# Block sums of the squared ReLU formed and stored by the first feed-forward product

## The chip, the cores and the metric

The kernel runs on one core of a Trainium2 chip. Its time is the device time of one execution in microseconds. Five engines work side by side: TensorE (matrix products), VectorE and ScalarE (element by element), GpSimd (also called POOL in the profile) and SyncE (SP), which here issues every transfer between the core's memory and the chip's large memory.

## The reference

One trunk layer of a streaming encoder on an input of 1024 frames with 1024 channels: an RWKV-7 branch and a convolution branch, merged under gates, and then a feed-forward part. Only that last part is touched:

```python
h2 = _rmsnorm(x, norm_ff_g[l])
x = x + jnp.square(jax.nn.relu(h2 @ w_ff1[l])) @ w_ff2[l]   # 1024 -> 4096 -> 1024 channels
return _rmsnorm(x, norm_final_g)
```

The second product sums over the 4096 hidden channels, so their order is free as long as the rows of `w_ff2` follow it.

## The kernel before

Everything is kept with the channels across the 128 partitions and the frames along them. A tile is 128 channels by 1024 frames; most instructions take half of one, 128 x 512. Float32 values are multiplied as two parts: `parts_of_` (L1306) lets ScalarE write the first part and VectorE or GpSimd the second, the low one, as the difference. A product of two such numbers is three matmuls. `low_engine` (L1302) gives every `lows[0]`-th low part to GpSimd and the rest to VectorE; in the second product `LOW4 = 3` makes it every third. The weights are split in `halved` (L1196), with the low part always on GpSimd.

Large products use seven block products instead of eight (`seven`, L1247). The right side is cut in two halves of its channels and two halves of the frames, B11, B12, B21 and B22, and the products need the differences T1 = B12 - B11, T2 = B22 - T1, T3 = B22 - B12 and T4 = B21 - T2 as well. In code `less` (L1313) forms one on VectorE. Weights have their own four sums (`weight_sums`, L1213), also on VectorE. A block product runs over four blocks of 128 x 128 weights and so takes twelve matmuls.

The first feed-forward product makes 32 tiles of hidden channels: four one by one (`single`, L1701), while the blocks of h are being formed in `h_blocks` (L1648), and 28 in fourteen pairs (`f_pair`, L1728). ScalarE applies ReLU and the square, and `store_f` (L1634) stores each half tile in `f_d`. Results lie in a pool of four work tiles (`wkt`, L1159).

The second product takes the hidden channels in eight groups of four tiles. `prepare` (L1759) loads the eight half tiles of a group, forms four differences for each of two pairs of tiles, and splits all blocks in two parts in `places`. `quad` (L1815) is the unit of work: seven products of twelve matmuls for four tiles of output; two quads make a group, and there are fourteen quads. VectorE adds every result to x, which lies in the tiles `C`. The eighth group is done directly (`last_group`, L1880), and needs its blocks without differences. The first group is prepared during the last pair (`last_pair`, L1740).

`prepare`, `h_blocks` and the like are generators in a list called `background`; one or two steps of the first in the list are traced after every three matmuls. `Count.until` (L1316) makes a step wait for a number of these. TensorE keeps the order in which the code is traced. The other engines did until line 1152, where `order_off` ends that; after it a scheduler at build time fixes their order from the dependencies and the trace order, so a transfer or a sum can be placed well ahead of the place where it is traced. At run time every engine, and SP with its transfers, goes through its own list in order.

Of the kernel before, what the change touches and what calls it, by code (L numbers as in the profile page):

```python
# [44 lines left out]
LOW4 = 3  # L45
# [49 lines left out]
def tile_hybrid_block(ctx: ExitStack, tc: tile.TileContext, xT, win, wap, wcp, wop, wf1, wf2,  # L95
# [3 lines left out]
    class Ordered:  # L99
        """While on, the instructions of an engine keep the order in which they are traced;  # L100
        work: how long they take, in ns."""
# [109 lines left out]
    def load_weight(src):  # L211
        """src: DRAM AP [128, 4, 128]; the transfer, then (second call) the split into two
        float32r parts whose sum it is."""
        raw = wp.tile([P, 4, P], F32, tag="raw", name="raw")
        sync.dma_start(raw, src)

        def halve():
            hi = wp.tile([P, 4, P], F32R, tag="whi", name="whi")
            lo = wp.tile([P, 4, P], F32R, tag="wlo", name="wlo")
            act.activation(hi, raw, AF.Copy)  # L220
            eng = pool if nload[0] % 2 else dve
            nload[0] += 1
            eng.tensor_tensor(out=lo, in0=raw, in1=hi.bitcast(F32), op=ALU.subtract)
            return hi, lo

        return halve
# [9 lines left out]
    def stream(pick):  # L236
        """Matrix products unit after unit, the weights of a part loaded ahead[0] parts before
        and split ahead[1] parts before; yields True after every three products, False when no
        unit can start. pick() names the next unit, WAIT for none now, None at the end. A unit:
        (wsrc [128, 8, 128] in DRAM, rhs(kt, seg) -> (hi, lo), evac(seg, psum), segs, what to  # L240
        trace after which of its yields), or a function that returns the list of its parts, or
        one that returns a generator (its first two steps load and prepare). A part: what traces
        its load and returns what traces its split; the generator of its products from the split
        weights, which yields what follows. What follows a product on other engines is traced
        after the next products."""
# [54 lines left out]
        def fetch():  # L300
            """Entries ahead of the one in work, no more than one of them WAIT."""
# [53 lines left out]
    def pick():  # L355
        """The first of the queue whose time has come."""
# [26 lines left out]
    def rms_scale(acc, eps):  # L383
        """acc [128, SEG], per-partition partial sums of squares, becomes 1/sqrt(mean + eps) on all partitions."""
# [29 lines left out]
    def early_unit(n):  # L414
        """Gate logits of the first half of the frames from x with its gain; then the scale of the frames."""
# [102 lines left out]
    H0, H1 = slice(0, 64), slice(64, 128)  # L518
    with ExitStack() as st:
# [17 lines left out]
        # ----- low-rank branches: first layer, the token shift folded into the weights  # L537
# [51 lines left out]
        def decay_and_a():  # L589
# [3 lines left out]
            # the two parts of the second layer's weights stacked over the contraction  # L593
# [54 lines left out]
        # ----- r, k, v with their token shift  # L648
# [26 lines left out]
        # ----- one step: head pair p, token segment s; i = 2 p + s  # L675
# [17 lines left out]
        # the parts of a step are generators: one stage a tick, a stage uses what other  # L693
        # engines made in the stages before
# [146 lines left out]
        # inverse of I - L: the 16 x 16 diagonal blocks by substitution, one block a partition  # L841
        def invert(i):
# [48 lines left out]
            # the blocks of 32 and of 64 from their halves  # L891
# [30 lines left out]
        # then the blocks of 32 and of 64 from their halves  # L922
# [11 lines left out]
        def chain(i):  # L934
            """The chunks of a step one after another; yields after each group of products."""
# [88 lines left out]
        # ----- conv branch and the merge gates  # L1024
# [25 lines left out]
        def conv(p, u):  # L1050
            """The even and the odd frames are each a filter of 16 taps over the even frames of u
            and one of 15 over the odd ones; what the odd frames need follows from the filter of
            the sums over the sum of both, less the two products that the even frames need."""
# [37 lines left out]
        # ----- the order of the products: chains of small ones among the large  # L1091
# [79 lines left out]
    # work of the other engines, traced in small steps between the products  # L1171
# [14 lines left out]
    # Two halves of the rows B of the right side (its channels) and of its columns (the frames):  # L1186
    # T1 = B12 - B11, T2 = B22 - T1, T3 = B22 - B12, T4 = B21 - T2; of the weights, by pairs of
    # tiles of output channels: S1 = A21 + A22, S2 = S1 - A11, S3 = A11 - A21, S4 = A12 - S2.
    # The products in their order: A11 B11, S1 T1, S2 T2, A12 B21, S3 T3, S4 B22, A22 T4.
    # seven places, each for a block of four tiles of half the frames in two parts  # L1190
# [5 lines left out]
    def halved(src, eng=pool):  # L1196
        """Two float32r parts of [128, 4, 128] whose sum is src."""
# [8 lines left out]
    def raw_tile(n):  # L1206
        """The n-th of eight places [128, 4, 128] for weights."""
# [5 lines left out]
    def weight_sums(srcs, base):  # L1213
        """What traces the loads and what the splits of the weights of the seven products."""
# [32 lines left out]
    def seven(srcs, base, blocks, pairs, evacs, hook):  # L1247
        """Parts of a unit: the seven products of one pair of tiles (or of two of half as many channels)."""
# [3 lines left out]
        # two pairs: the sums that are done at once before those that stay  # L1252
# [21 lines left out]
    def four(emit, place):  # L1274
        """What follows each of the seven products; emit(tile, half of the frames, place or None, values)."""
# [30 lines left out]
    def parts_of_(z, src):  # L1306
        """Generator: src as the sum of its two parts z."""
# [8 lines left out]
    class Count:  # L1316
        """Yields of the products so far; hooks wait for them."""
# [14 lines left out]
    # conv: LayerNorm, swish, block sums  # L1332
# [4 lines left out]
    def conv_branch():  # L1337
# [44 lines left out]
        for j in range(4):  # L1382
            for kt in (j, 4 + j):
                # c_d has the even frames, then the odd ones; from here on in order
# [42 lines left out]
    # A  # L1427
# [29 lines left out]
    # A @ W_A under its gate  # L1457
# [33 lines left out]
    # the merged branches: y in the places of C  # L1491
# [15 lines left out]
    def y_blocks():  # L1507
        """The block sums of y, as their places and the last tiles of y come."""
        B = [C[j] + C[4 + j] for j in range(4)]     # b11, b12, b21, b22; then t2, t3, t4, b22
# [61 lines left out]
    # x1 = x + y @ W_out, in the same places  # L1571
# [24 lines left out]
    # the first hidden channels come from x1 under its gain, the scale of the frames later  # L1596
# [34 lines left out]
    f_d = [dtile(f"f_d{i}", [P, T]) for i in range(4 * NK)]  # L1631
    FO = (4, 5, 6, 0, 2, 1, 3)

    def store_f(i, s, t):  # L1634
        sync.dma_start(f_d[i][:, s * SEG : (s + 1) * SEG], t)
# [12 lines left out]
    def h_blocks():  # L1648
# [30 lines left out]
        for j in range(4):  # L1679
            yield from parts_of_(FP[6][j], C[4 + j][0])  # L1680
        yield from at_F.until(16 * NCL + 56)
        for m in range(NK):
            for h in range(NSEG):
                sync.dma_start(C[m][h], x1_d[m][:, h * SEG : (h + 1) * SEG])
                yield

# [14 lines left out]
    def single(i):  # L1701
        """Parts of a tile of hidden channels, the last frames first."""
# [25 lines left out]
    def f_pair(n, i, hook):  # L1728
        def emit(j, s, t, src):
            if t is None:  # L1730
                t = wkt("c21")
# [4 lines left out]
        return lambda: pair(wf1, n, i, i + 1, [PL[z] for z in FO], emit, lambda i, s: wkt("c"), hook)()  # L1736
# [3 lines left out]
    def last_pair():  # L1740
        if at_L.n == 0:
            drain()
            lows[0] = LOW4
            background.append(prepare(0))
        at_L.hook()
# [4 lines left out]
    # back to the channels of x, 4 tiles of the hidden channels at a time  # L1750
    NG = 8
# [7 lines left out]
    def prepare(g):  # L1759
        """The blocks of group g of hidden channels, of two tiles each; of the last group B11, B12, B21, B22."""  # L1760
        z = places(g)
        FB[g] = [[(z[4 * j + 2 * k], z[4 * j + 2 * k + 1]) for k in range(2)] for j in range(7)]
        raw = {}

        def load(k):
            for a, kk in ((1, k), (2, 2 + k)):
                for s in range(NSEG):
                    t = raw[k, a, s + 1] = wkt("fl") if g and k == 0 else flt("fl")
                    sync.dma_start(t, f_d[4 * g + kk][:, s * SEG : (s + 1) * SEG])

        def free(i):
            """The place of block i of group 0 has been read by the last products of the hidden channels."""
            return at_L.until(4 * (i // 2 + 1) if g == 0 else 0)

        load(0)
        yield
        if g:
            load(1)
            yield
        for k in range(2):  # L1780
            if k == 1 and g == 0:
                load(1)
                yield
            b11, b12, b21, b22 = (raw[k, a, s] for a in (1, 2) for s in (1, 2))
# [193 lines left out]
```

## Time and profile before

| | us |
|---|---|
| median of 3 runs (2221.46 to 2228.85) | 2223.68 |
| span of the profiled execution, first to last instruction | 2220.0 |
| TensorE busy in it | 2075.3 (93%) |
| VectorE busy | 1617.9 (73%) |
| ScalarE busy | 1120.3 (50%) |
| GpSimd busy | 898.0 (40%) |

The profile is of one execution. Busy time is a sum over the whole span, so a stage in which VectorE has no idle time does not show in it; windows do that. In rows, PE is TensorE, DVE is VectorE, ACT is ScalarE; `c<-c,x` means that the instruction writes a tile named c from a tile c and a tile x. Names repeat with the tile pools: `place` and `a` are the places of the blocks, `fl` and `c` tiles loaded from `f_d` or the tiles of x, `cmean` two more tiles of x, `raw` and `s` weights and their sums, `x` and `g` the accumulators of TensorE. In windows, PEclk is the granted TensorE clock as a share of 2.4 GHz.

### The profile page before, as it was taken

To read this page: it belongs to the slowest core of one execution; us is meant where nothing else is said; L and a number is where in the kernel's file an instruction comes from. 1 tells how busy PE (TensorE), PEld (TensorE's weight loads), DVE (VectorE), ACT (ScalarE), POOL (GpSimd) and SP (SyncE) were. 2 spreads that over 40 slices of the span, in tenths; PEclk is the share of its full clock that TensorE was granted. 3 is DMA by queue.
4 is the path that set the end of the run, shared out by engine and by line. 5 is a ranking of instruction groups with operands and counts; after the bars stand their busy time and mean duration, and the time that the engine had idled before them with its cause. 6 is when DMAs were issued, how large, how long until landed. Compare 5 with 4: busy or idle time off the path is not lost. (4 is left out here: it accounts for less than half of the span.)

```text
span 2220.0 us, 35280 instructions
## 1 busy us (share of the span) xinstructions
PE 2075.3 (93%) x12806; PEld 1554.3 (70%) x12806; DVE 1617.9 (73%) x2781; ACT 1120.3 (50%) x2102; POOL 898.0 (40%) x1026
## 2 busy tenths in 40 slices
PE   6999999999999999999989989799899998889897
PEld 4757666767676666676666778577688876667686
DVE  8435889869778888898484987979432249998865
ACT  7454555555555555654323753455555555333323
POOL 4103333333333333342112245665545456566641
PEclk8999999999999999999999999999899999999999
DMA  5243222222222222232254355242433334233212
GB/s 180 90 158 79 62 73 53 80 65 78 78 66 79 72 81 72 74 87 82 70 178 159 128 170 163 95 137 93 169 105 114 105 106 151 91 95 105 85 49 76
DMA packets 223358, 224.87 MB, mean 101 GB/s; under 512 B 113488, under 2 KB 131408, under 8 KB 223184
## 3 DMA queue, kind: packets, MB, share of 16 engines
q1 hardware_dynamic: 223184, 222.62, 32.3%
q8 instruction: 101, 1.65, 0.3%
q14 instruction: 73, 0.60, 0.1%
HBM read 155.96 MB, written 66.60 MB: 100 GB/s over the span
## 5 line engine op out<-in xcount | busy, mean ns | idle before, releaser
L114 POOL TENSOR_TENSOR wlo<-raw,whi 128x512 fp32r<-128x512 f32 x258 | 369.4, 1434 | 698.9 <-ACT whi L114 640.1
L114 PE MATMUL g<-hhi,whi 128*128 128x512 f32 x912 | 402.9, 442 | 0.0
L114 PE MATMUL g<-hhi,wlo 128*128 128x512 f32 x912 | 363.4, 398 | 2.1 <-POOL wlo L114 1.5
L114 PE MATMUL g<-hlo,whi 128*128 128x512 f32 x912 | 364.8, 400 | 0.0
L114 ACT ACTIVATE whi<-raw 128x512 fp32r<-128x512 f32 x328 | 204.5, 625 | 222.4 <-PE g L114 73.0
L114 PEld LDWEIGHTS g<-hhi,whi 128*128 128x128 f32 x912 | 173.1, 190 | 52.4 <-issue 6.0
L114 PE MATMUL x<-place,whi 128*128 128x512 f32 x608 | 195.5, 403 | 14.8 <-DVE cmean L114 7.8
L114 PE MATMUL x<-a,whi 128*128 128x512 f32 x544 | 177.2, 408 | 33.3 <-ACT c L114 11.3
L114 PE MATMUL g<-place,whi 128*128 128x512 f32 x624 | 198.8, 399 | 7.6 <-ACT place L114 4.1
L114 PEld LDWEIGHTS g<-hhi,wlo 128*128 128x128 f32 x912 | 174.4, 191 | 44.5 <-POOL wlo L114 2.4
L114 PE MATMUL g<-a,whi 128*128 128x512 f32 x624 | 196.9, 397 | 5.7 <-DVE c L114 3.3
L114 PEld LDWEIGHTS g<-hlo,whi 128*128 128x128 f32 x912 | 174.1, 191 | 26.6 <-issue 1.9
L114 DVE TENSOR_TENSOR c<-c,g 128x512 f32<-128x512 f32 (+1 forms) x131 | 84.6, 650 | 94.8 <-PE g L114 94.6
L114 PEld LDWEIGHTS x<-a,whi 128*128 128x128 f32 x544 | 105.2, 196 | 63.0 <-ACT c L114 12.7
L114 PEld LDWEIGHTS x<-place,whi 128*128 128x128 f32 x608 | 115.1, 192 | 48.1 <-issue 6.2
L114 POOL TENSOR_TENSOR wlo<-s,whi 128x512 fp32r<-128x512 f32 x72 | 107.5, 1495 | 100.1 <-ACT whi L114 91.8
L114 PEld LDWEIGHTS g<-place,whi 128*128 128x128 f32 x624 | 118.2, 190 | 38.6 <-ACT place L114 5.0
L114 PEld LDWEIGHTS g<-a,whi 128*128 128x128 f32 x624 | 117.7, 190 | 35.7 <-DVE c L114 4.6
L114 POOL TENSOR_TENSOR tmpb<-lb,xb 64x15 f32<-64x15 f32 (+7 forms) x240 | 110.2, 459 | 79.3 <-DMA lb<-scr_l 63.2
L114 ACT ACTIVATE stw<-stv,wc 64x64 f32<-64x64 f32 x240 | 82.6, 344 | 97.7 <-DVE stv L114 94.2
L114 PE MATMUL g<-a,wlo 128*128 128x512 f32 x312 | 123.4, 396 | 5.6 <-POOL wlo L114 5.2
L114 PE MATMUL g<-place,wlo 128*128 128x512 f32 x312 | 123.6, 396 | 1.6 <-POOL wlo L114 1.6
(286 smaller groups left out, 4327.6 us busy)
## 6 DMA issues: line engine op xcount, KB each, us to landing
raw<-wf SPq DMA_DIRECT2D x128, 256.0 KB, 2.8
raw<-win SPq DMA_DIRECT2D x124, 256.0 KB, 3.1
f_d<-c SPq DMA_DIRECT2D x56, 256.0 KB, 2.0
fl<-f_d SPq DMA_DIRECT2D x46, 256.0 KB, 2.9
c<-f_d SPq DMA_DIRECT2D x18, 256.0 KB, 3.3
xt<-xT SPq DMA_DIRECT2D x16, 256.0 KB, 5.3
ga_d<-gt SPq DMA_DIRECT2D x16, 256.0 KB, 2.1
z_d<-za SPq DMA_DIRECT2D x16, 256.0 KB, 2.0
```

The lines of the kernel that those rows point to most:

```text
L114: ins = f(*a, **k)
```

## The change

`f_d` becomes one tensor for each pair of tiles, with a place for every block: B11, T1, T2, B21, T3, B22, T4. `store_f` stores B11, B21 and B22 as they come; once all four halves of a pair are there, `f_sums` is put at the head of the background. After four steps it forms the four differences in place on VectorE, one a step, and stores each. For the last group the four blocks alone are stored. `prepare` loads each block ready made and only splits it, block by block in the order of use, with loads six blocks ahead (three in the first group). `LOW4` is so large that all of its low parts go to VectorE.

The results of the pairs come to lie in a ring of eight tiles, those of C[4] to C[7], instead of the four work tiles, as soon as `h_blocks` has ended; x1 is loaded back into these eight during the last pair, and only into C[0] to C[3] at the earlier place. A group's two tile pairs are now neighbours, so the rows of `w_ff2` are permuted on the host.

```diff
-LOW4 = 3
+LOW4 = 1 << 30
...
-    f_d = [dtile(f"f_d{i}", [P, T]) for i in range(4 * NK)]
+    NP = 2 * NK
+    NG = 8
+    f_d = [dtile(f"f_d{k}", [7 if k // 2 < NG - 1 else 4, P, SEG]) for k in range(NP)]
     FO = (4, 5, 6, 0, 2, 1, 3)
+    FT = [{} for _ in range(NP)]
 
     def store_f(i, s, t):
-        sync.dma_start(f_d[i][:, s * SEG : (s + 1) * SEG], t)
+        k, a = divmod(i, 2)
+        f = FT[k]
+        f[a, s] = t
+        if k // 2 == NG - 1:
+            sync.dma_start(f_d[k][2 * a + s], t)
+            return
+        if (a, s) != (0, 1):
+            sync.dma_start(f_d[k][{(0, 0): 0, (1, 0): 3, (1, 1): 5}[a, s]], t)
+        if len(f) == 4:
+            background.insert(0, f_sums(k))
+
+    def f_sums(k):
+        b11, b12, b21, b22 = (FT[k][a, s] for a in range(2) for s in range(2))
+        for _ in range(4):
+            yield
+        for n, out, x, y in ((1, b11, b12, b11), (4, b12, b22, b12), (2, b22, b22, b11), (6, b21, b21, b22)):
+            less(out, x, y)
+            sync.dma_start(f_d[k][n], out)
+            yield
...
+        ring.extend(C[m][h] for m in range(4, NK) for h in range(NSEG))
         yield from at_F.until(16 * NCL + 56)
-        for m in range(NK):
+        yield from x1_back(range(4))
+
+    ring = []
+
+    def x1_back(ms):
+        for m in ms:
             for h in range(NSEG):
                 sync.dma_start(C[m][h], x1_d[m][:, h * SEG : (h + 1) * SEG])
                 yield
+
+    def ft():
+        if not ring:
+            return wkt("c")
+        ring.append(ring.pop(0))
+        return ring[-1]
...
             if t is None:
-                t = wkt("c21")
+                t = ft()
...
-        return lambda: pair(wf1, n, i, i + 1, [PL[z] for z in FO], emit, lambda i, s: wkt("c"), hook)()
+        return lambda: pair(wf1, n, i, i + 1, [PL[z] for z in FO], emit, lambda i, s: ft(), hook)()
...
             drain()
+            ring.clear()
             lows[0] = LOW4
             background.append(prepare(0))
+            background.append(x1_back(range(4, NK)))
...
+        items = [(j, k) for j in range(7 if g < NG - 1 else 4) for k in range(2)]
         raw = {}
+        LA = 6 if g else 3
+
+        def load(n):
+            j, k = items[n]
+            raw[n] = wkt("fl") if g and n % 2 else flt("fl")
+            sync.dma_start(raw[n], f_d[2 * g + k][j])
+
+        for n in range(LA):
+            load(n)
         yield
...
+        yield
+        for n, (j, k) in enumerate(items):
+            if n + LA < len(items):
+                load(n + LA)
+
+            yield from at_L.until(4 * (j // 2 + 1) if g == 0 else 0)
+            yield from parts_of_(FB[g][j][k], raw.pop(n))
...
-        "wop": wl(a(w_out)[0]), "wf1": wl(a(w_ff1)[0]), "wf2": wl(a(w_ff2)[0]),
+        "wop": wl(a(w_out)[0]), "wf1": wl(a(w_ff1)[0]), "wf2": wl(a(w_ff2)[0].reshape(8, 2, 2, P, 1024).transpose(0, 2, 1, 3, 4).reshape(4096, 1024)),
```

## Rows read from the trace of the kernel before

**Rows 1.** Windows: from:to, length, busy us (count) of each engine, clock, DMA share, GB/s.

```profile
1504.91:1568.82 63.91, 53.31 (x208) 40.82 (x206) 57.33 (x61) 36.59 (x63) 33.99 (x23) 0.87 0.32 107
1584.83:1817.19 232.36, 232.36 (x1010) 189.33 (x1008) 68.14 (x85) 126.81 (x216) 111.43 (x84) 1.00 0.32 109
1817.19:1840.06 22.87, 19.89 (x85) 15.63 (x84) 16.81 (x20) 15.20 (x29) 13.85 (x9) 1.00 0.36 119
1840.06:2157.16 317.10, 286.90 (x1177) 222.49 (x1176) 276.64 (x366) 116.74 (x205) 194.06 (x133) 0.97 0.30 96
2118.91:2157.16 38.25, 38.25 (x169) 31.54 (x168) 25.58 (x38) 11.98 (x20) 20.88 (x16) 1.00 0.17 56
```

**Rows 2.** Waits of TensorE, fourteen quads: total us, times, longest.

```profile
PE x L114 <- DVE cmean L114: 12.8, 6, 3.9
PE g L114 <- DVE c L114: 4.3, 4, 1.8
...
PE x L114 <- DVE c L114: 3.5, 5, 1.6
```

**Rows 3.** Waits of TensorE from the single tiles to the end of the first pair.

```profile
PE x L114 <- ACT c L114: 7.6, 1, 7.6
```

**Rows 4.** Instruction groups of VectorE, fourteen quads: busy us, mean ns, idle before.

```profile
L114 DVE TENSOR_TENSOR place<-fl,place 128x512 fp32r<-128x512 f32 x28 | 26.2, 940 | 0.8 <-ACT place L114 0.8
L114 DVE TENSOR_TENSOR a<-fl,a 128x512 fp32r<-128x512 f32 x21 | 23.7, 1129 | 0.0
L114 DVE TENSOR_TENSOR fl<-fl 128x512 f32<-128x512 f32 x24 | 22.3, 928 | 0.6 <-POOL place L114 0.6
L114 DVE TENSOR_TENSOR raw<-raw,raw 128x512 f32<-128x512 f32 x14 | 17.8, 1268 | 5.4 <-POOL wlo L114 5.4
L114 DVE TENSOR_TENSOR raw<-raw,s 128x512 f32<-128x512 f32 x14 | 16.2, 1157 | 3.8 <-POOL wlo L114 3.8
L114 DVE TENSOR_TENSOR s<-s,raw 128x512 f32<-128x512 f32 x13 | 14.0, 1077 | 0.0
L114 DVE TENSOR_TENSOR s<-raw 128x512 f32<-128x512 f32 x13 | 12.2, 936 | 17.4 <-POOL wlo L114 10.3 <-DMA raw<-wf 7.1
L114 DVE TENSOR_TENSOR fl<-c,fl 128x512 f32<-128x512 f32 x12 | 10.3, 857 | 0.0
...
L114 DVE TENSOR_TENSOR place<-c,place 128x512 fp32r<-128x512 f32 x10 | 8.7, 874 | 0.0
L114 DVE TENSOR_TENSOR fl<-fl,fl 128x512 f32<-128x512 f32 x6 | 5.9, 982 | 0.0
L114 DVE TENSOR_TENSOR c<-c,fl 128x512 f32<-128x512 f32 x7 | 5.2, 749 | 0.0
L114 DVE TENSOR_TENSOR a<-c,a 128x512 fp32r<-128x512 f32 x4 | 3.5, 881 | 0.0
```

**Rows 5.** Instruction groups of GpSimd, fourteen quads: low parts of blocks alone.

```profile
L114 POOL TENSOR_TENSOR place<-fl,place 128x512 fp32r<-128x512 f32 x14 | 21.1, 1512 | 14.4 <-ACT place L114 13.4 <-PE x L114 0.8
L114 POOL TENSOR_TENSOR a<-fl,a 128x512 fp32r<-128x512 f32 x11 | 16.4, 1490 | 14.0 <-ACT a L114 11.2 <-DVE fl L114 1.8 <-PE x L114 0.9
L114 POOL TENSOR_TENSOR place<-c,place 128x512 fp32r<-128x512 f32 x5 | 6.6, 1314 | 6.2 <-ACT place L114 6.2
...
L114 POOL TENSOR_TENSOR a<-c,a 128x512 fp32r<-128x512 f32 x2 | 3.0, 1515 | 0.7 <-ACT a L114 0.7
```

**Rows 6.** Instruction groups of VectorE, twelve pairs of the first product.

```profile
L114 DVE TENSOR_TENSOR s<-s,raw 128x512 f32<-128x512 f32 x12 | 21.4, 1784 | 0.0
...
L114 DVE TENSOR_TENSOR s<-raw 128x512 f32<-128x512 f32 x12 | 8.3, 693 | 19.7 <-DMA raw<-wf 19.7
```

**Rows 7.** Transfers of the tensor f_d, the same twelve pairs, all stores.

```profile
DMA to landing us min/median/max: 2.0/2.0/3.6
```

**Rows 8.** Waits of the SP queue, fourteen quads.

```profile
SPq L114 <- POOL wlo L114: 140.1, 42, 10.1
```

**Rows 9.** Waits of VectorE, fourteen quads.

```profile
DVE s L114 <- DMA raw<-wf: 7.1, 3, 4.5
```

More of the change, by code (lines that the diff above doesn't have):

```diff
@@ L1748, in tile_hybrid_block @@
         program.append(f_pair(n, i, at_F.hook if i < 30 else last_pair))
-    NG = 8
     ODD = NCL // 2 % 2
@@ L1762, in prepare @@
         FB[g] = [[(z[4 * j + 2 * k], z[4 * j + 2 * k + 1]) for k in range(2)] for j in range(7)]
+        items = [(j, k) for j in range(7 if g < NG - 1 else 4) for k in range(2)]
         raw = {}
[L1765 to L1775, printed above, removed]
-        yield
[L1777 to L1784, printed above, removed]
-            if g == NG - 1:
-                for j, b in enumerate((b11, b12, b21, b22)):
-                    yield from parts_of_(FB[g][j][k], b)
-                continue
-            yield from free(0)
-            yield from parts_of_(FB[g][0][k], b11)
-            t1 = b11
-            less(t1, b12, b11)
-            yield
-            yield from free(1)
-            yield from parts_of_(FB[g][1][k], t1)
-            less(b12, b22, b12)
-            yield
-            t2 = t1
-            less(t2, b22, t1)
-            yield
-            yield from free(2)
-            yield from parts_of_(FB[g][2][k], t2)
-            yield from free(3)
-            yield from parts_of_(FB[g][3][k], b21)
-            less(b21, b21, t2)
-            yield
-            yield from free(4)
-            yield from parts_of_(FB[g][4][k], b12)
-            yield from free(5)
-            yield from parts_of_(FB[g][5][k], b22)
-            yield from free(6)
-            yield from parts_of_(FB[g][6][k], b21)
+        LA = 6 if g else 3
[5 more added lines that the diff above has]
+            load(n)
+        yield
+        yield
[4 more added lines that the diff above has]
+            yield from parts_of_(FB[g][j][k], raw.pop(n))
     def quad(g, q):
```

## The prediction

> **What bounds the kernel now.** I read the page first. TensorE is busy nearly everywhere, so only the stages where it loses time can give any back. So the next view was a table of windows, cut where the timeline of matmuls shows a unit of seven products begin [rows 1]. Its five lines are: the four single tiles of the first feed-forward product and the first two products of its first pair; twelve of its fourteen pairs; its last pair; the fourteen quads of the second product; and the last two quads alone. The reader is to see three things.
>
> The first product runs without a gap: twelve pairs in 232.36 us, 19.36 us each, with TensorE busy throughout at clock 1.00 (2.4 GHz) and VectorE busy for only 68.14 us [rows 1].
>
> The second product has as many matmuls in a quad as a pair has, and takes 317.10 us for fourteen. At 19.36 us each it would take 271.1, so 46.0 us are lost, part of them as a lower clock (mean 0.97) after stalls. VectorE is busy for 276.64 of the 317.10 us, 87.2% [rows 1]. The waits of TensorE there name VectorE's accumulations into the rows of x (12.8, 4.3 and 3.5 us) ahead of anything else [rows 2]. The check is the last two quads: there only eight blocks are prepared, and those of the last group without differences; VectorE falls to 25.58 of 38.25 us and the two quads run at 19.1 us each [rows 1]. So VectorE is the bound of the second product, and it stops being one somewhere between 67% and 87%.
>
> Around the second product two more places lose time: the last pair takes 22.87 us, 3.5 over [rows 1], and the change from single tiles to pairs has one stall of 7.6 us, on ScalarE's copy out [rows 3]. In that stretch VectorE is busy for 57.33 of 63.91 us [rows 1].
>
> **The change part by part.** *Differences leave the second product.* VectorE forms them today from the loaded tiles: 24, 12, 6 and 7 instructions that write fl or c from fl and c, 43.7 us in the stretch of fourteen quads [rows 4]. (There are 56; the other seven fall in the last pair.) All go: -43.7 us of VectorE.
>
> *Every low part goes to VectorE.* In the same stretch GpSimd does 14 + 11 + 5 + 2 = 32 of them, 47.1 us [rows 5]. VectorE's own 63 cost 26.2 + 23.7 + 8.7 + 3.5 = 62.1 us, 0.986 each [rows 4]. A moved one costs between 0.69 us, which a subtraction takes when nothing holds it (0.693), and 1.78 us, which the one that starts beside a GpSimd instruction takes in the first product (1.784) [rows 6]. I take 0.986, the same operation in the same stage: 32 x 0.986 = +31.5 us.
>
> *Less collision.* VectorE's weight sums have a mean of 1.08 to 1.27 us where most are long and 0.94 where they are not [rows 4], against 0.69 free [rows 6]: 54 of them (60.2 us) lose 22.9 us. The 63 low parts lose 62.1 - 63 x 0.69 = 18.6, and the 49 differences 43.7 - 33.8 = 9.9. Together 51.4 us beside 133 GpSimd instructions [rows 1], 0.39 us for each. With 32 fewer: -12.5 us. The bounds are 0 and twice that.
>
> Sum for VectorE: -43.7 + 31.5 - 12.5 = -24.7 us, so 276.6 becomes 251.9. At the busy share of today (87.2%) the stretch takes 251.9 / 0.872 = 289 us, 28 less. The bounds: all moved parts held and no relief, -43.7 + 57.0 = +13.3, which is 15 us longer; none held and double relief would put it below TensorE's 271.1, so at most 46.0 shorter. I take 29, a little over the sum, because ScalarE's first parts no longer stand behind a difference on VectorE.
>
> The Trainium skill, on the page SBUF — State Buffer, section Who interferes with whom, has the rule behind these two prices: a VectorE instruction with two SBUF inputs and a GpSimd instruction that reads SBUF exclude one another, and the second one waits for the whole of the first. The trace agrees (0.693 against 1.784). Read strictly it speaks against this change: the moved parts join the side that waits, while the weights' low parts stay on GpSimd. That is the second rival below.
>
> *The last pair.* The preparation of the first group goes on there, and loses its seven differences; its low parts on GpSimd come over. I take -2 of the 3.5 us that are lost; 0 and 3.5 are the ends.
>
> *Differences enter the first product.* Twelve pairs get four each, 48 instructions, 33 us at 0.69 and 85 at 1.78 [rows 6]. VectorE is idle there for 232.36 - 68.14 = 164 us [rows 1], in gaps behind TensorE's products, so I cost them at nothing. They write in place, over tiles whose plain store must have landed: 2.0 us in the median, 3.6 at most [rows 7]. If VectorE sits in such a wait, an accumulation behind it is late and a bank is not freed; the ring of eight tiles and the four steps of delay are the cover. If it is gone, a pair loses about one product, 19.36 / 7 = 2.8 us, 33 us over twelve pairs. GpSimd's 84 weight parts (111.43 us [rows 1]) can be held too; they have as much room again. Nothing below zero is to be had, since TensorE has no gap there.
>
> *The single tiles.* Two pairs of tiles get their differences while the blocks of h are formed: eight more instructions, 5.5 us at 0.69 to 14.2 at 1.78, in a stretch with 63.91 - 57.33 = 6.6 us of idle VectorE [rows 1], on the path to the stall of 7.6 us [rows 3]. Also, all four work tiles are held until the differences are stored, and the first pair's copy takes one of them. Ends: 0 and +14. I take +6, close to the free price. Against it, eight of the sixteen reloads of x1 leave that stretch for the end of the first product; I count nothing for them.
>
> *Transfers.* Six more quarter-megabyte transfers a group each way on the SP queue. DMA share is 0.30 to 0.32 now [rows 1], so bytes cost nothing; the order of the queue is the third rival. The weight rows are permuted on the host: nothing.
>
> Sum: -29 - 2 + 0 + 6 = -25 us on a span of 2220.0, so 2195. The median of the runs shown lies 3.7 above that span, which gives **2199 us**.
>
> **The rivals.** *TensorE becomes the bound.* VectorE's load falls far enough that the second product and the last pair run without gaps, as the last two quads do now [rows 1]: -46.0 - 3.5 and no cost at the single tiles, 2174 us. For it: a group then has no chain of differences between load and block. Against it: 251.9 us of VectorE in 271.1 is 93%, more than today's share.
>
> *VectorE stays the bound.* The lock takes back what the count gives: moved parts at 1.2 us, halfway between the two prices [rows 6], and no relief, -43.7 + 38.4 = -5.3, 6 us gained. The single tiles cost the same 6, and the last pair gains nothing: 2224 us. For it: the count falls only from 366 to 349 instructions. Against it: the same operation costs 0.986 now, with more GpSimd work beside it.
>
> *The SP queue turns the second product slower.* A group has fourteen block loads instead of eight between its eight weight loads. A block load waits until the low part that last read its tile is done; all those are now on the busiest engine, and a weight load queued behind it comes late. SP already waits for 140.1 us on GpSimd's weight parts, and VectorE's sums wait for a weight load 3 times, 7.1 us in all, 4.5 the longest [rows 8, 9]. It decides from 25 / 14 = 1.8 us a quad. At 2.4 us, the mean of those three, fourteen quads lose 33 and the change ends 8 above the median, 2232 us; at 4.5 it is 2262. Against it: eight tiles and six loads ahead, and ScalarE and VectorE need no chain before they free one. The Trainium skill, on the page DMA: Bandwidth & Descriptors, section Anatomy of one DMA — SWDGE (gpsimd) path, says that the wait for a semaphore happens on the issuing sequencer before dispatch; by it every load behind the waiting one is held, as this rival needs.
>
> *The first product is no longer free,* and the differences only move the loss: 33 us, as worked out above, so 2199 + 33 = 2232 us.
>
> **How the numbers follow.** Forecast 0.52 (2188 to 2212), TensorE bound 0.18, VectorE still bound 0.15, SP queue 0.10, first product held 0.05. A change of 0.3% is 6.7 us, about what can be told from none here. Faster by more: the forecast, the first rival and a third of the second, 0.75. Slower by more: most of the last two, 0.13. The rest, 0.12, is no change. The range reaches from the TensorE bound to just past the second rival, 2176 to 2228.
>
> **What would show it.** Right: quads of the middle groups at 20 to 21 us instead of 22 to 24, VectorE near 250 us in the second product with no instruction that writes fl from fl, GpSimd at about 101 instructions, pairs still at 19.4 us. The step of the single tiles is right if the stall before the first pair grows by about 6 us and wrong if it shrinks. The price of a moved part is read from the mean of VectorE's low parts: near 1.0 or below supports the sum, 1.2 or more the second rival. Gaps in the pairs, or sums that wait for weight loads in most quads, would make the prediction wrong.

## The result, and the profile after

The changed kernel takes 2190.38 us in the median (2188.81 to 2192.52, 4 runs) against 2222.57 for the kernel before beside it: ratio 0.9862, 95% interval 0.9839 to 0.9885. Run again with later experiments it gave 2187.1 us, ratio 0.9852 (0.9829 to 0.9874). The forecast was 2199 us in a range of 2176 to 2228.

The spans of the profiled executions, 2220.0 and 2187.1 us, differ by 32.9 us. Cut at the same units of work as [rows 1], they compare like this:

| stage | before, us | after, us | difference | forecast |
|---|---|---|---|---|
| up to the single tiles | 1504.91 | 1504.92 | 0.0 | 0 |
| single tiles and first pair | 79.92 | 84.22 | +4.3 | +6 |
| twelve pairs | 232.36 | 232.40 | 0.0 | 0 |
| last pair | 22.87 | 23.63 | +0.8 | -2 |
| fourteen quads | 317.10 | 279.43 | -37.7 | -29 |
| last group and end | 62.84 | 62.50 | -0.3 | 0 |

Of the 37.7 us that the quads gain, 25.6 are idle time of TensorE that is gone; the other 12.0 are TensorE's own time for the same matmuls, 286.90 us [rows 1] and 274.87 now, with a mean granted clock of 0.97 before and 0.99 after.

The windows of the changed kernel, cut as in [rows 1] and with the same columns (the busy times are TensorE, its weight loads, VectorE, ScalarE, GpSimd):

```profile
1504.92:1573.71 68.79, 52.57 (x208) 40.80 (x206) 61.27 (x68) 36.88 (x63) 38.20 (x24) 0.90 0.34 115
1589.14:1821.54 232.40, 232.40 (x1009) 189.56 (x1008) 130.65 (x132) 126.80 (x216) 114.76 (x84) 1.00 0.45 153
1821.54:1845.17 23.63, 21.49 (x85) 16.81 (x84) 17.02 (x23) 18.66 (x34) 8.46 (x7) 0.93 0.82 266
1845.17:2124.60 279.43, 274.87 (x1178) 221.41 (x1176) 248.96 (x343) 114.79 (x199) 143.23 (x101) 0.99 0.46 140
```

In the second line VectorE goes from 68 to 131 us and TensorE still has no gap. In the fourth VectorE is at 248.96 us with 343 instructions and GpSimd at 101 instructions; the forecast had 251.9 and 101. Of the fourteen quads the first three take 20.7, 23.8 and 21.9 us, all others 19.1 to 19.8: from the fourth on, TensorE is the bound. The loss before was not even either. The first three quads, before and after, with the same columns:

```profile
1840.06:1917.09 77.03, 65.78 (x253) 49.24 (x252) 71.19 (x89) 32.56 (x58) 48.90 (x33) 0.93 0.40 130
1845.17:1911.56 66.39, 61.83 (x254) 47.79 (x253) 62.27 (x81) 29.41 (x52) 32.77 (x22) 0.97 0.62 195
```

The very first quad took 31.2 us before, with a wait of TensorE of 3.9 us for VectorE in it and a mean granted clock of 0.84 (the two levels are 1.2 and 2.4 GHz, 0.50 and 1.00). Now it takes 20.7. So 10.5 of the 37.7 us were won in the first quad, and 27.1 in the eleven after the third, where TensorE is now busy without a gap.

TensorE's waits in all fourteen, where [rows 2] had 20.6 us on VectorE:

```profile
PE x L114 <- DVE c L114: 3.1, 2, 1.9
PE x L114 <- DVE cmean L114: 0.9, 2, 0.6
PE g L114 <- DVE c L114: 0.5, 1, 0.5
```

VectorE's groups of instructions in the same stretch, low parts and weight sums, to be laid beside [rows 4]:

```profile
L114 DVE TENSOR_TENSOR place<-fl,place 128x512 fp32r<-128x512 f32 x41 | 41.0, 1002 | 0.4 <-ACT place L114 0.4
L114 DVE TENSOR_TENSOR a<-fl,a 128x512 fp32r<-128x512 f32 x27 | 28.2, 1044 | 0.1
L114 DVE TENSOR_TENSOR s<-s,raw 128x512 f32<-128x512 f32 x13 | 15.4, 1182 | 0.0
L114 DVE TENSOR_TENSOR raw<-raw,s 128x512 f32<-128x512 f32 x14 | 13.2, 945 | 2.0 <-POOL wlo L114 2.0
L114 DVE TENSOR_TENSOR place<-c,place 128x512 fp32r<-128x512 f32 x15 | 12.6, 844 | 0.2 <-ACT place L114 0.2
L114 DVE TENSOR_TENSOR raw<-raw,raw 128x512 f32<-128x512 f32 x13 | 9.7, 746 | 2.9 <-POOL wlo L114 2.9
...
L114 DVE TENSOR_TENSOR s<-raw 128x512 f32<-128x512 f32 x12 | 9.3, 777 | 7.8 <-DMA raw<-wf 4.0 <-POOL wlo L114 3.8
L114 DVE TENSOR_TENSOR a<-c,a 128x512 fp32r<-128x512 f32 x9 | 7.7, 858 | 0.1
```

No line writes fl from fl any more. The 92 low parts cost 89.5 us, 0.97 each, where 0.986 was taken. The last column tells of something that the forecast didn't weigh: idle time before a weight sum that ends with a weight's low part on GpSimd was 10.3 + 5.4 + 3.8 = 19.5 us [rows 4] and is 8.7 us now (11.8 in a second profile of the changed kernel).

### The profile page after: what moved, and what is told of

It is laid out like the page before. It is cut to its first block, busy times and chain, and to the rows that moved or that the text cites. A ratio compares the mean times of both kernels' runs of the same rounds, so it can differ in the third digit from the quotient of the medians.

```text
span 2187.1 us, 35495 instructions
## 1 busy us (share of the span) xinstructions
PE 2064.7 (94%) x12806; PEld 1555.9 (71%) x12806; DVE 1661.1 (76%) x2816; ACT 1121.9 (51%) x2102; POOL 846.7 (39%) x991
## 5 line engine op out<-in xcount | busy, mean ns | idle before, releaser
L114 ACT ACTIVATE whi<-raw 128x512 fp32r<-128x512 f32 x328 | 204.9, 625 | 240.1 <-PE g L114 93.5
L114 DVE TENSOR_TENSOR c<-c,c 128x512 f32<-128x512 f32 x90 | 100.7, 1126 | 31.0 <-ACT c L114 16.3
```

What stands on the lines that cost most here:

```text
L114: ins = f(*a, **k)
```

## The experiments

Each took away, put back or added one thing. The two numbers to follow are the length of the fourteen quads and VectorE's busy time in them.

**One half without the other.** Only the differences moved, the low parts shared as before:

```diff
-LOW4 = 1 << 30
+LOW4 = 3
```

> The changed kernel with every third low part of the second product on GpSimd again (as before the change); the differences stay in the first product. Theory (VectorE's load is what counted): VectorE loses about 31 us of low parts there, gets some 12 us back as collisions, falls to about 230 us in the fourteen quads, and TensorE stays the bound: quads 271 to 278 us, whole 2183 to 2191 us, no slower than the changed kernel. Rival (GpSimd's block parts were the harm: its weight parts queue behind them and VectorE waits for the port): most of the gain goes again, over 2205 us.

Measured: 2192.36 us, ratio 0.9878 (0.9849 to 0.9907). The other half alone, in the kernel before:

```diff
-LOW4 = 3
+LOW4 = 1 << 30
```

> The kernel before with the other half alone: all low parts of the second product on VectorE, differences still formed there. Theory (VectorE's load): plus 31.5 for moved parts, minus 12.5 for collisions, so 295 us of VectorE in the fourteen quads, 332 us at 89% busy instead of 317: about 2239 us. Rival (GpSimd's block parts were the harm): faster than before, 2200 to 2215 us.

Measured: 2212.18 us, ratio 0.9961 (0.9941 to 0.9981). The windows of the fourteen quads, first with the differences alone moved, then with the low parts alone moved:

```profile
1845.01:2131.36 286.35, 275.97 (x1177) 220.90 (x1176) 238.72 (x316) 116.16 (x202) 187.15 (x133) 0.99 0.44 138
```

```profile
1838.02:2143.97 305.95, 283.75 (x1178) 218.25 (x1177) 293.37 (x396) 116.11 (x201) 148.82 (x101) 0.99 0.31 99
```

Taking the differences out is worth 30.7 us alone (317.1 to 286.4). Moving the low parts is worth 11.2 us alone, although VectorE's load goes up from 276.6 to 293.4 us: the load was foreseen (295), the time was not (332). VectorE is busy for 95.9% of the stretch in place of 87.2%; before the last two quads it has no idle time at all (267.7 of 267.7 us). What it waited for before is gone. This is VectorE's group there that carried most of that wait in [rows 4]:

```profile
L114 DVE TENSOR_TENSOR s<-raw 128x512 f32<-128x512 f32 x13 | 12.4, 954 | 0.0
```

So neither theory held whole. GpSimd's block parts did harm, and the differences did more.

Where the 11.2 us were won is seen in the first three quads of the kernel with the low parts alone moved:

```profile
1838.02:1904.35 66.33, 60.87 (x253) 46.34 (x252) 66.33 (x90) 28.99 (x51) 32.73 (x22) 1.00 0.42 137
```

They take 10.7 us less than before, 4.9 of them as shorter time of TensorE for the same matmuls, at a granted clock of 1.00 in place of 0.93. The other eleven quads take 239.6 us, and 240.1 before: there 21.6 us more of VectorE's work went into its idle time and won nothing. With the differences gone it is the other way round. The first three quads take 66.1 us with the low parts shared and 66.4 with them moved, the other eleven 220.2 and 213.0. Why GpSimd's block parts cost most at the start before, and later on once the differences are gone, stays open.

**VectorE's load put back without its chain.** After its two parts are made, a loaded tile is subtracted from itself, in place, and nothing reads the result:

```diff
-            yield from parts_of_(FB[g][j][k], raw.pop(n))
+            t = raw.pop(n)
+            yield from parts_of_(FB[g][j][k], t)
+            if g < NG - 1 and n % 7 < 4:
+                less(t, t, t)
```

> The changed kernel with eight subtractions more for each of the first seven groups, each over a loaded tile once its two parts are made; nothing reads what they write, so only VectorE's time and the port are loaded, with no chain from load to block. Theory (load): 249 + 56 x 0.92 = 300 us of VectorE at 89% busy, 337 us instead of 279 less what falls in the last pair: about 2240 us. Rival (the chain load, difference, first part, low part was the harm, not the count): VectorE can fill up, 300 / 0.98 = 306, about 2212 us.

Measured: 2224.78 us, no better than before the change (1.0029, 1.0014 to 1.0044). Half as many:

```diff
-            if g < NG - 1 and n % 7 < 4:
+            if g < NG - 1 and n % 7 in (1, 3):
```

> The changed kernel with four subtractions more for each of the first seven groups instead of eight. Theory (a ceiling: with GpSimd at weights alone VectorE can be busy for 95% of the quads, and below that TensorE is the bound): 249 + 23 = 272 us of VectorE, 272 / 0.95 = 286 us, 7 more than the changed kernel. Rival (every microsecond of VectorE's load delays TensorE in proportion): halfway between 279.4 and 311.7, so 295 us.

Measured: 2209.52 us, ratio 0.9931 (0.9904 to 0.9958). The fourteen quads, with eight a group, then with four:

```profile
1855.33:2167.04 311.71, 284.74 (x1178) 219.76 (x1176) 296.06 (x391) 115.91 (x199) 145.16 (x100) 0.99 0.41 125
```

```profile
1838.31:2135.08 296.77, 279.66 (x1178) 220.99 (x1176) 275.48 (x367) 114.51 (x199) 144.98 (x100) 0.99 0.42 131
```

From 249.0 to 275.5 and 296.1 us of VectorE the quads grow from 279.4 to 296.8 and 311.7: 0.66 us for each us of load, and 0.69 over both steps. That is neither today's share kept (337) nor a ceiling below which load is free (286). The proportional rival, 295, came nearest. But the rate is a mean over unlike quads, and the share of 95% behind the 286 had the last two quads in it, where VectorE has little to do. The first twelve quads alone, with none, four and eight a group:

```profile
1845.17:2086.34 241.17, 236.61 (x1009) 189.84 (x1008) 223.36 (x306) 102.79 (x179) 122.33 (x85) 0.99 0.50 153
1838.31:2096.82 258.51, 241.40 (x1009) 189.46 (x1008) 249.88 (x330) 102.51 (x179) 124.05 (x84) 0.99 0.46 142
1855.33:2128.78 273.45, 246.48 (x1009) 188.22 (x1008) 270.47 (x354) 103.91 (x179) 124.67 (x84) 0.99 0.44 134
```

VectorE's idle time shrinks from 17.8 to 8.6 to 3.0 us: the added load goes in part into idle time and in part into the length. With four a group, 6.8 us of what is left idle is waiting for weight loads, so the loads have a part in that number.

With the same load as four a group (276.6 against 275.5) the kernel before needs 20.3 us more; this part is not VectorE's load. Nor does it go with the chain from load to difference to block alone: the kernel with only the low parts moved keeps that chain and takes 305.95 us at 293.4 us of load, less than the 311.7 at 296.1 without it. Of the things that differ, GpSimd's block parts are what is left.

**GpSimd's work put back without its blocks.** In the kernel before with all low parts on VectorE, GpSimd gets subtractions that nothing reads:

```diff
-LOW4 = 3
+LOW4 = 1 << 30
...
+                if n[0] % 11 == 5:
+                    idle_sub(FB[g][n[0] // 11][0][0][:, 0:NCONST].bitcast(F32))
```

> The kernel before with all low parts on VectorE (305.9 us for the fourteen quads), with 42 subtractions of 128 x 448 added on GpSimd in the quads, over first parts that are long ready, nothing reads them: about the port time of the 32 low parts that went, without their waits and without delay to any block. Theory (collisions at the port): VectorE's load grows by some 13 us from 293 and the quads are back at 317 us or above. Rival (GpSimd's list in order: weight parts stood behind block parts that waited for ScalarE): 304 to 310 us.

Measured: 2231.23 us, ratio 1.0032 (1.0012 to 1.0053).

```profile
1845.68:2168.26 322.58, 288.44 (x1178) 219.49 (x1177) 302.54 (x397) 116.29 (x201) 193.50 (x137) 0.98 0.30 94
```

36 of the 42 lie in the quads, which grow by 16.6 us over the kernel with the low parts alone moved; VectorE's busy time grows by 9.2, or 0.25 us for each of them. So GpSimd's work beside VectorE's counts, as the theory has it. But it isn't all. VectorE's waits for weight parts on GpSimd grow as well, without the 42 and with them:

```profile
DVE raw L114 <- POOL wlo L114: 2.0, 2, 1.2
```

```profile
DVE raw L114 <- POOL wlo L114: 9.0, 5, 3.1
```

The added instructions themselves stood waiting for ScalarE's first parts, with weight parts behind them, so they were not as free as meant:

```profile
L114 POOL TENSOR_TENSOR dummy<-place 128x448 f32<-128x448 f32 x18 | 22.7, 1259 | 10.5 <-ACT place L114 9.9
L114 POOL TENSOR_TENSOR dummy<-a 128x448 f32<-128x448 f32 x18 | 20.8, 1153 | 18.0 <-ACT a L114 11.9 <-DVE s L114 3.7 <-PE g L114 1.0
```

By VectorE's record, 9.2 of the 16.6 us are longer instructions and 7.0 longer waits for GpSimd's list.

**The cover of the first product.** Without the ring, results stay in the four work tiles:

```diff
-        ring.extend(C[m][h] for m in range(4, NK) for h in range(NSEG))
```

> The changed kernel without the ring of eight tiles: the results of the pairs stay in the four work tiles. Theory (the ring is what keeps the first product free): a copy waits until a difference of the pair before is stored and landed (2.1 us), 1 to 3 us in each of twelve pairs, so 2200 to 2226 us. Rival (the four steps of delay and VectorE's gaps are enough): 2187 to 2194 us, pairs still at 19.4 us.

Measured: 2202.14 us, ratio 0.9918 (0.9891 to 0.9944). The twelve pairs, and TensorE's waits from there to the end of the last pair:

```profile
1587.13:1836.47 249.34, 235.98 (x1010) 188.42 (x1008) 123.83 (x133) 127.76 (x218) 116.25 (x84) 1.00 0.40 140
```

```profile
PE x L114 <- ACT c L114: 13.4, 12, 1.2
```

The pairs cost 16.9 us more than with the ring, with one stall in each. The ring is a cover that is needed, and the price without it is half of the 33 us that the forecast named. The four steps of delay were not tested.

**The single tiles.** Two edits take differences out of that stretch. One makes the single tiles the last group, so that the last two pairs get differences instead (the second product's weights are rolled by one group to match):

```diff
-        if k // 2 == NG - 1:
+        if k < 2:
...
-            sync.dma_start(raw[n], f_d[2 * g + k][j])
+            sync.dma_start(raw[n], f_d[(2 * g + k + 2) % NP][j])
```

> The changed kernel with the four single tiles as the last group, which needs no differences (the hidden channels and the rows of the second weights are permuted for it); the last two pairs get differences in their place. Theory (the eight differences on VectorE cost what the stretch of single tiles grew by, 4.5 us): the stall before the first pair falls from 12.3 to about 7.6 us and the first of the twelve pairs begins at about 1585 us as before the change; the last pair and the first quad pay 1 to 3 us for eight differences there: 2186 to 2190 us. Rival (the stall comes from GpSimd and the port): it stays at 12 us, and the whole gets slower by those 1 to 3.

The other forms the second four after the blocks of h:

```diff
-            t = wkt("fr")
+            t = flt("fr") if i >= 2 else wkt("fr")
...
-            background.insert(0, f_sums(k))
+            background.insert(len(background) if k == 1 else 0, f_sums(k))
```

> The changed kernel with the differences of the second two single tiles formed after the blocks of h, from four tiles of their own instead of the work tiles. Theory (half of the 4.5 us are these four differences and the copy that waits for their tiles): the stall before the first pair falls by 2 to 3 us, 2187 to 2189 us; the first four differences still cost their part. Rival (only the first four matter, which delay the blocks): no change.

Measured: 2190.79 us, ratio 0.9856 (0.9821 to 0.989), and 2188.75, ratio 0.9856 (0.9833 to 0.9878). The stretch from the single tiles to the end of the first pair takes 84.2 us in the changed kernel, 80.0 and 82.0 in these two, and 79.9 before. (The growth is thus 4.3 us; the expectations have 4.5.) In the second edit a stretch at the lower granted clock, 0.50 or 1.2 GHz, that follows two waits of TensorE, falls for the most part ahead of the cut. Counted from 24 matmuls earlier, with these waits inside, that edit saves 1.0 us and the first 4.2. TensorE's longest wait there, in the changed kernel and in the first edit:

```profile
PE x L114 <- ACT c L114: 12.3, 1, 12.3
```

```profile
PE x L114 <- ACT c L114: 8.3, 1, 8.3
```

So the eight differences, with the stores and the work tiles that hang on them, are what the stretch grew by. But the first edit gives it back: its quads take 286.0 us, 6.5 more. Four of its eight differences fall in the last pair and four in the first quad; the first three quads grow by 3.6 us and the other eleven, which have none, by 3.0, and for these no cause is shown.

**The last pair.** The first group's blocks in the eight tiles of the ring (`spare`), seven ahead:

```diff
+            spare.extend(ring)
...
-        LA = 6 if g else 3
+        LA = 6 if g else 7
...
-            raw[n] = wkt("fl") if g and n % 2 else flt("fl")
+            raw[n] = spare[n % 8] if g == 0 else wkt("fl") if n % 2 else flt("fl")
```

> The changed kernel with the blocks of the first group loaded into the eight ring tiles, seven ahead, instead of four tiles, three ahead; the reloads of x1 into these tiles follow later by themselves. Theory (in the last pair ScalarE stands in order before a block that has not landed, and a copy out waits behind it): last pair from 23.6 to 20 to 21 us, the first three quads from 66.4 to 60 to 63, whole 2180 to 2186 us. Rival (VectorE's load in the last pair and the first group is what costs): within 2 us of the changed kernel there.

Measured: 2191.73 us, ratio 0.9866 (0.9833 to 0.99); the last pair takes 22.9 us instead of 23.6 and the first three quads 65.3 instead of 66.4. That is less than the theory asked for, and it is not landing either: TensorE's waits in the last pair are 2.6 us, where the changed kernel has 2.1, but its granted clock is 1.00 in place of 0.93. The changed kernel itself, profiled again, had 24.0 and 65.9.

**Put together.** Differences of the last two pairs formed from their stored blocks in the third and fourth group, with the single tiles as the last group and the wide loads, both as above:

```diff
+    def late_sums(k):
+        FT[k] = {}
+        for n, j in (((0, 0), 0), ((0, 1), 1), ((1, 0), 3), ((1, 1), 5)):
+            FT[k][n] = flt("fl") if sum(n) % 2 else wkt("fl")
+            sync.dma_start(FT[k][n], f_d[k][j])
+        yield
+        yield from f_sums(k)
...
+                    if g in (2, 3):
+                        background.append(late_sums(NP - 4 + g))
```

> The changed kernel with the single tiles as the last group, the differences of the last two pairs formed from their stored blocks in the third and fourth group of the second product, and the first group's blocks loaded into the ring tiles. Theory (what the differences cost depends on where VectorE has room: none beside the single tiles and in the last pair and first group, some from the third group on): first pair at 1550 us of the span as before the change, last pair and first three quads 1 to 3 us shorter, at most 2 us for the eight differences in the quads: 3 to 6 us under the changed kernel run beside it. Rival (no room anywhere in the second product): the eight differences and their loads cost there what they save, within 2 us of it.

Beside it the changed kernel, unedited:

> The changed kernel as it is, on the same chip for comparison: 2186 to 2194 us.

Measured on one chip: 2190.02 us, ratio 0.9851 (0.9827 to 0.9875), and 2187.1 for the changed kernel. The stages before the quads came out as expected (79.5 us to the end of the first pair, last pair 22.8), but the quads took 8.6 us more than in the first profile of the changed kernel, where VectorE's load grew by 7.4:

```profile
1837.91:2125.90 287.99, 276.38 (x1177) 218.88 (x1176) 256.38 (x350) 113.41 (x196) 140.71 (x101) 1.00 0.49 151
```

The rival was right: in the third and fourth group the differences cost what they save. VectorE's waits for weight loads grew at the same time, from 4.0 to 9.2 us, so the eight loads and eight stores that came with the differences may have a part in it. At last the two small edits together, the later sums of the single tiles and the eight tiles of the first group:

```diff
+            background.insert(len(background) if k == 1 else 0, f_sums(k))
...
+        LA = 6 if g else 7
...
+            raw[n] = spare[n % 8] if g == 0 else wkt("fl") if n % 2 else flt("fl")
```

> The changed kernel with two edits that each saved a little in their own stage: the differences of the second two single tiles after the blocks of h, from tiles of their own (2.2 us less from the single tiles to the end of the first pair), and the first group's blocks loaded seven ahead into the ring tiles (1.7 us less in the last pair and the quads). Theory (the stages add up): about 4 us under the changed kernel, 2183 to 2187 us. Rival (what one stage saves moves the order that the scheduler makes in the next): within 2 us of it, 2187 to 2190 us.

Measured: 2185.32 us, ratio 0.9834 (0.9804 to 0.9863). The intervals overlap with those of the changed kernel, and its stages show 1.5 us saved at the single tiles, 0.5 in the quads and none in the last pair. No version here is shown to beat the changed kernel.

## Why the prediction was right, and where it was off

*VectorE's load in the quads* was the step that carried the forecast, and it held: 251.9 us foreseen, 248.96 measured. The three terms are visible in it: no differences, low parts at 0.97, and weight sums down from 60.2 us for 54 to 47.6 for 52. The second rival had the moved parts at 1.2 us and the other low parts as before, which is a mean of 1.06 over all of them; with 0.97 it fell. Of the 92 low parts 47 began while GpSimd was working and took 1.26 us in the mean, the other 45 took 0.68. The lock in the Trainium skill (page SBUF — State Buffer, section Who interferes with whom) is thus seen in this trace, but about half of the low parts never met it.

*From load to time* is where it was off. "At the busy share of today (87.2%) the stretch takes 251.9 / 0.872 = 289 us": it took 279.4. The share is no property of VectorE. It was 87% with GpSimd's block parts among its weight parts and 96% without them, in kernels that differ in nothing else. So the price of the moved parts had the wrong sign in time: +19 us of load, which alone made the stretch 11.2 us shorter, nearly all of it in the first three quads. That the sum came near is in part luck. By the forecast's rule the differences were worth 43.7 / 0.872 = 50 us, and the moved parts with their relief cost 19.0 / 0.872 = 22. Taken out first, the differences gave 30.7 us; the parts, moved then, gave 7.0 more. Two errors, of 19 us one way and 29 the other, leave one of 9. The stretch gained 37.7 us in place of 29, and the first rival, TensorE as the bound, holds from the fourth quad on.

*The single tiles* were forecast at +6 and cost +4.3, for the reason given: with the eight differences gone from there the stretch is back at 80.0 us.

*The first product* stayed free, and the ring was rightly named as its cover. VectorE does wait in order for plain stores to land there, 13.0 us in ten waits, and TensorE, busy for all of the 232.40 us, shows nothing late behind it:

```profile
DVE c L114 <- DMA f_d<-c: 13.0, 10, 2.6
```

*The last pair* was forecast at -2 and came at +0.8. ScalarE's waits there, before and after:

```profile
ACT a L114 <- DVE fl L114: 4.4, 2, 3.1
ACT c L114 <- DVE c L114: 2.6, 1, 2.6
ACT a L114 <- DMA fl<-f_d: 1.7, 1, 1.7
ACT a L114 <- DMA c<-f_d: 1.0, 1, 1.0
```

```profile
ACT c L114 <- DVE c L114: 4.0, 3, 3.1
ACT a L114 <- DMA fl<-f_d: 1.8, 2, 1.1
ACT a L114 <- DMA c<-f_d: 1.1, 2, 0.9
```

The wait for the differences is gone, as forecast. The copies wait longer for VectorE, 4.0 us in place of 2.6, and the wait for blocks that have not landed is about as it was, 2.9 in place of 2.7, although the DMA share went from 0.36 to 0.82 with the reloads of x1. TensorE's idle time fell from 3.0 to 2.1 us. What turned the sign is the clock: after a wait of 1.9 us the granted clock drops to 0.50 for a while, 0.93 in the mean of the stretch where it was 1.00 [rows 1], and TensorE's own time for the same matmuls goes from 19.89 to 21.49 us. Before the change that drop came in the first quad.

The first three quads still lose some 8 us against 19.36 each. In the second of them VectorE has no idle time (23.8 of 23.8 us, 31 instructions where the quads after it, up to the last two, have 25 to 27) and the mean clock is 0.93. Why the work gathers there stays open.

*The SP queue* didn't turn against the change: SP waits for VectorE's low parts now, 107.7 us in all in the quads, but the waits of VectorE's sums for weight loads went from 7.1 to 4.0 us, and to 1.4 in the second profile.

## What to carry to other kernels

Count an engine's load by stage from rows, and move work to the stage where it is idle: 49 subtractions took 44 us of VectorE where it was nearly full; of the 56 in their new place, the 48 beside an idle VectorE cost no time, and the eight beside a busy one cost 4.3 us. Don't turn load into time with today's busy share; find what the idle time of the busy engine waits for, because moving that work can pay even when it adds load. And test the parts of a change one by one, also when the sum comes out: here two terms were off in opposite ways. Look at a stretch unit by unit before you divide its loss by the number of units; over a quarter of the gain in the quads lay in one of fourteen. Where an engine is within about a tenth of full, added load still costs in part: 0.66 us for each us here, as a mean over quads with and without idle time.

## What the runs showed of the hardware

VectorE's additions that take one input from an accumulator kept a mean of 675 to 678 ns over the fourteen quads in every kernel here, whatever GpSimd did. In the fourteen quads of the changed kernel, VectorE's additions and subtractions of two tiles ranged from 0.68 to 1.80 us, with a mean of 0.97 for the low parts. All 62 of them that took over 0.72 us began while GpSimd was working, and of the 85 others two did; of the 195 additions from an accumulator 93 did, and none of the 195 took over 0.69 us. An added GpSimd subtraction of 128 x 448 cost VectorE 0.25 us, less than the 0.39 that the forecast drew from [rows 1, 4].
